# A kernel for a two-layer decoder trunk: the weights of the down and output products begin 128 bytes further on

## The chip, the cores and the metric

The kernel runs on 1 core of one Trainium2 chip. The metric is the device time of one execution in microseconds (us), as the median of several runs. A change within 0.2%, 1.2 us here, can't be told from none.

## What is computed

Two layers of a decoder over 256 tokens of 1024 numbers. Layer 0 mixes the tokens by stick-breaking attention, layer 1 by block-sparse attention with rotary positions (with 256 tokens its one block is plain causal attention). Behind each stands a squared-ReLU MLP. Cut to what matters here:

```python
def squared_relu_mlp(x, w1, w2):
    return jnp.square(jax.nn.relu(x @ w1)) @ w2

for i in range(DEPTH):                      # 2
    ln1_g, ln1_b, w1, w2, ln2_g, ln2_b = channel[i]
    h = layer_norm(DEEPNORM_ALPHA * h + mixers[i % N_MIXERS](h), ln1_g, ln1_b)
    h = layer_norm(DEEPNORM_ALPHA * h + squared_relu_mlp(h, w1, w2), ln2_g, ln2_b)
```

Each mixer ends in `merge_blocks(o) @ w_o`, the output projection. w1 is 1024 x 4096, w2 is 4096 x 1024, w_o 1024 x 1024, all float32.

## The kernel before, in words

Each float32 operand is split into a high and a low part (float32r), and a product is three matmuls into one accumulator: high by high, high by low, low by high (mm3, line 193). A matmul holds a block of 128 x 128 of one operand in the array, the weights, or stationary operand (sta), and streams the other, the moving operand (mov), past it. In the trace a matmul reads out<-moving,stationary.

All weights of the model come as units of 128 x 4 x 512 (1 MB): SyncE's queue loads a unit into a raw tile, ScalarE casts it to hi, VectorE subtracts to get lo (split, line 202). Which role hi and lo play depends on the product:

- Query and key products of layer 0 (qkT_ps) and six of eight chunks of the first MLP matrix (up_ps, up, line 638) run in projT (line 329): the weights are slices of hi and lo, the moving operand is xh or xl, 256 tokens, 256 columns.
- The other projections (v_ps, qk_ps, and two chunks of up_ps) run in proj (line 322): the weights are slices of xh and xl, the moving operand is hi or lo, 512 columns.
- The output projection (wo_ps, wo, line 596) takes its weights from oh and ol, the attention's output, and the down products with the second MLP matrix (dn_ps, down, line 670) theirs from hh and hl, the squared hidden values. The moving operand is hi or lo, 512 columns; only the last 24 matmuls of the kernel stream 256 columns.

hh, hl, oh and ol are the tiles of the pool st (line 167), three buffers of 4096 bytes per partition under each of two tags. A stationary slice is 128 numbers, 512 bytes per partition, and all slices of a tile lie a multiple of 512 bytes apart, so they all begin at the same place modulo 512. So do the moving slices, which are 1024 or 2048 bytes apart.

Pools lie behind one another in the order in which they are made, and a tile takes its size rounded up to 32 bytes. `shift` (line 215) puts an unused tile of a given size into the pool one; GAP (line 30) has its two sizes, 224 ahead of xh and 288 behind v. The layout that comes of it, as the first byte modulo 512:

| tiles | begins at, modulo 512 | role |
|---|---|---|
| xh, xl, h, v | 352 | moving in projT, stationary in proj |
| const (the identity in it) | 416 | moving in transposes |
| raw, hi, lo | 416 | moving in proj, wo, down; stationary in projT |
| ten buffers of t2k (qk, r, and others) | 416, 448, 480, 0, 32, 64, 96, 128, 160, 192 | stationary in transposes and scores |
| four buffers of t3k | 224, 256, 288, 320 | stationary in transposes |
| pt | 352 | moving in the attention's last product |
| st: hh, hl, oh, ol | 352 | stationary in down and wo |
| small tiles sm, sma | various | scalars per row |

The order of all instructions is fixed while the program is built by Plan (line 64), a small model that gives each operation a cost and emits it where its engine is free first. Its costs are constants per size; it knows no address. In the MLP the loop at line 698 takes up(c) and down(c - 2) in turn: 96 matmuls of 256 columns, then 48 of 512.

Of the kernel before, what the change touches and what calls it, by code (L numbers as in the profile page):

```python
# [7 lines left out]
F32 = mybir.dt.float32  # L8
# [6 lines left out]
P = 128  # L15
# [11 lines left out]
SEQ = (("A0", "V0", "A1", "A2", "A3", "V1"), ("A0", "A1", "V0", "A2", "A3", "V1"))  # L27

RAWS, LIVE = 3, 5
GAP = (224, 288)  # L30
N2K, N3K, NPT = 10, 4, 4
MARGIN, WINDOW = 0.5, 0.25
X_LOADS = {0: 1, 1: 1, 2: 2, 4: 2, 6: 2}
# [121 lines left out]
def trunk(ctx: ExitStack, tc: tile.TileContext, x, xt, cst, cstb, w, ln, out):  # L155
    nc = tc.nc

    def pool(name, bufs, **kw):
        return ctx.enter_context(tc.tile_pool(name=name, bufs=bufs, **kw))
# [4 lines left out]
    t2k = pool("t2k", N2K)  # L164
    t3k = pool("t3k", N3K)
    pts = pool("pts", NPT)
    st = pool("st", 3)
    small = pool("small", 4)
    smalla = pool("smalla", 8)
# [45 lines left out]
    def shift(n):  # L215
        one.tile([P, n // 4], F32, tag=f"gap{n}", name=f"gap{n}")

    shift(GAP[0])
    xh = one.tile([P, KT, T], F32R, tag="xh", name="xh")
    xl = one.tile([P, KT, T], F32R, tag="xl", name="xl")  # L220
    h = [one.tile([P, D], F32, tag=f"h{t}", name=f"h{t}") for t in range(NT)]
    v = [one.tile([P, D], F32, tag=f"v{t}", name=f"v{t}") for t in range(NT)]
    shift(GAP[1])

# [584 lines left out]
```

## Time and profile before

| | |
|---|---|
| median of 3 runs | 604.55 us (604.28 to 605.46) |
| profiled execution | 603.84 us, span 602.1 us |
| busy: TensorE, its weight loads, VectorE, ScalarE, GpSimd | 98%, 84%, 65%, 48%, 4% of the span |
| the chain that ended last | 95% TensorE |
| mean granted clock of TensorE | 0.995 |
| read from HBM | 107.71 MB, 181 GB/s over the span |

The profile is of one execution. Engines are named PE (TensorE, its matmuls), PEld (its weight loads), DVE (VectorE), ACT (ScalarE), POOL (GpSimd), SP (SyncE). L191 is line 191 of the kernel, and since mm records every matmul of the projections there, they are told apart by tiles. A matmul's record lasts longer than its turn, for matmuls are pipelined: what a matmul costs in a stream is the time from its start to the next one's start.

### The profile page before, as it was taken

What the parts mean: (1) busy time and instruction counts of PE and PEld (TensorE: products, weight loads), DVE (VectorE), ACT (ScalarE), POOL (GpSimd) and SP (SyncE); (2) the same over time, 40 slices, a digit from 0 to 9 for tenths busy, and PEclk for the clock granted to TensorE, in tenths of its full rate; (3) what the DMA queues carried; (4) which work ended last, traced back from release to release, by engine and by line L of the source; (5) the groups of instructions that cost most, each with busy time, mean ns of one, the idle gap of its engine ahead of it and who ended that gap; (6) DMA issues with size and microseconds to landing.
All of it is one profiled execution on the core that took longest, in us unless ns stands there. A gap on an engine that the chain in (4) does not pass through costs nothing.

```text
span 602.1 us, 8790 instructions
## 1 busy us (share of the span) xinstructions
PE 591.5 (98%) x3652; PEld 507.1 (84%) x3652; DVE 389.7 (65%) x492; ACT 290.5 (48%) x419; POOL 24.6 (4%) x30
## 2 busy tenths in 40 slices
PE   8999999999999999999999999999999999999994
PEld 6899987879899899898877777778798998899883
DVE  5877874878455554655879787668667537446454
ACT  5866663436443543642536655626346426435400
POOL 0000000000000000000122022000000000000000
PEclk9999999999999999999999999999999999999998
DMA  8994335185546337337274443443764464365101
GB/s 310 393 334 143 126 154 200 70 277 169 215 179 269 149 143 279 140 144 275 71 249 170 145 144 132 140 141 101 249 260 162 149 270 169 157 235 209 72 0 70
DMA packets 17895, 109.31 MB, mean 182 GB/s; under 512 B 1984, under 2 KB 2624, under 8 KB 5824
## 3 DMA queue, kind: packets, MB, share of 16 engines
q1 hardware_dynamic: 17856, 108.76, 49.0%
q8 instruction: 28, 0.46, 0.3%
q14 instruction: 11, 0.09, 0.0%
HBM read 107.71 MB, written 1.05 MB: 181 GB/s over the span
## 4 chain that ended last, share of the span: by engine, by line
PE 95%; DVE 2%; ACT 1%; DMA 1%; SPq 0%; issue 0%; DVEq 0%; ACTq 0%
PE dn_ps L191 29%; PE up_ps L191 28%; PE wo_ps L191 7%; PE v_ps L191 7%; PE qk_ps L191 7%; PE qkT_ps L191 7%; PE sc L191 3%; PE o L509 2%; PE xt L387 1%; PE tp L556 1%; DMA h<-in_xt 1%; DVE lo L206 1%; DVE xl L206 1%; PE ht_ps L663 1%; PE pt_ps L491 1%; PE pt_ps L493 1%
## 5 line engine op out<-in xcount | busy, mean ns | idle before, releaser
L206 DVE TENSOR_TENSOR lo<-raw,hi 128x1024 fp32r<-128x1024 f32 (+1 forms) x196 | 229.7, 1213 | 48.8 <-ACT hi L205 47.1
L205 ACT CAST hi<-raw 128x1024 fp32r<-128x1024 f32 (+1 forms) x196 | 192.0, 1032 | 64.2 <-issue 42.4
L191 PE MATMUL up_ps<-xh,hi 128*128 128x256 f32 x384 | 106.4, 277 | 0.0
L191 PE MATMUL up_ps<-xl,hi 128*128 128x256 f32 x384 | 106.2, 276 | 0.0
L191 PE MATMUL up_ps<-xh,lo 128*128 128x256 f32 x384 | 106.1, 276 | 0.0
L191 PE MATMUL dn_ps<-hi,hl 128*128 128x512 f32 (+1 forms) x260 | 101.5, 390 | 0.0
L191 PE MATMUL dn_ps<-lo,hh 128*128 128x512 f32 (+1 forms) x260 | 101.0, 388 | 0.0
L191 PE MATMUL dn_ps<-hi,hh 128*128 128x512 f32 (+1 forms) x260 | 100.2, 385 | 0.0
L191 PEld LDWEIGHTS up_ps<-xl,hi 128*128 128x128 f32 x384 | 72.1, 188 | 0.5
L191 PEld LDWEIGHTS up_ps<-xh,hi 128*128 128x128 f32 x384 | 72.1, 188 | 0.5
L630 DVE SCALAR_TENSOR_TENSOR r<-up_ps,r 128x512 f32<-128x512 f32 x32 | 22.0, 688 | 78.0 <-ACT r L628 78.0
L191 PEld LDWEIGHTS up_ps<-xh,lo 128*128 128x128 f32 x384 | 72.2, 188 | 0.0
L628 ACT ACTIVATE r<-up_ps 128x512 f32<-128x512 f32 x32 | 19.1, 596 | 95.0 <-PE up_ps L191 95.0
L191 PEld LDWEIGHTS dn_ps<-lo,hh 128*128 128x128 f32 x260 | 48.8, 188 | 10.5
L191 PEld LDWEIGHTS dn_ps<-hi,hh 128*128 128x128 f32 x260 | 48.8, 188 | 10.0
L191 PEld LDWEIGHTS dn_ps<-hi,hl 128*128 128x128 f32 x260 | 48.9, 188 | 9.4
L191 PE MATMUL qkT_ps<-xh,hi 128*128 128x256 f32 x128 | 36.8, 287 | 0.0
L191 PE MATMUL qkT_ps<-xh,lo 128*128 128x256 f32 x128 | 35.8, 280 | 0.2 <-DVE lo L206 0.2
L191 PE MATMUL qkT_ps<-xl,hi 128*128 128x256 f32 x128 | 35.7, 279 | 0.0
L205 ACT CAST xh<-xt 128x512 fp32r<-128x512 f32 x12 | 7.0, 587 | 42.9 <-PE xt L387 41.1
L191 PE MATMUL v_ps<-hi,xh 128*128 128x512 f32 x64 | 26.4, 413 | 0.0
L191 PE MATMUL qk_ps<-hi,xh 128*128 128x512 f32 x64 | 26.3, 411 | 0.0
(97 smaller groups left out, 885.8 us busy)
## 6 DMA issues: line engine op xcount, KB each, us to landing
raw<-in_w SPq DMA_DIRECT2D x64, 1024.0 KB, 5.0
raw<-in_wqkv SPq DMA_DIRECT2D x22, 1024.0 KB, 5.2
raw<-in_wo SPq DMA_DIRECT2D x8, 1024.0 KB, 4.8
raw<-in_first SPq DMA_DIRECT2D x8, 256.0 KB, 4.8
gb<-in_l_ln_g SPq DMA_DIRECT2D x4, 512.0 KB, 4.0
gb<-in_l_ln_b SPq DMA_DIRECT2D x4, 512.0 KB, 5.8
h<-in_x SPq DMA_DIRECT2D x2, 512.0 KB, 7.7
h<-in_xt SPq DMA_DIRECT2D x3, 256.0 KB, 4.8
```

Of the source, the lines that this page charges most:

```text
L191: nc.tensor.matmul(ps, sta, mov, start=start, stop=stop)
L205: f = lambda: nc.scalar.copy(hi(), src())
L206: g = lambda: nc.vector.tensor_tensor(lo(), src(), hi().bitcast(F32), op=ALU.subtract)
L387: nc.tensor.transpose(XB[t][:, n, k * P:(k + 1) * P], h[t][:, (4 * n + k) * P:(4 * n + k + 1) * P], ident)
L491: nc.tensor.transpose(ps[:, j, 0:P], pj[:, T:T + P], ident)
L493: nc.tensor.transpose(ps[:, j, T:T + P], pj[:, P:T], ident)
L509: nc.tensor.matmul(o[HD * j:HD * j + HD, 0, kt * P:T], v[kt][:, hd * HD:(hd + 1) * HD], pt[:, 0:T] if kt == 0 else pt[:, T:T + P], start=k ...
L556: nc.tensor.transpose(tb["tp"][:, pr, c0:c0 + P], QK[g, t]["qk"][:, e * T + pr * P:e * T + pr * P + P], ident)
L628: nc.scalar.activation(box["r", n], ps, AF.Relu)
L630: return dve(512, lambda: nc.vector.scalar_tensor_tensor(box["r", n], ps, 0.0, box["r", n], op0=ALU.max, op1=ALU.mult), after=[a], rank=0. ...
L663: nc.tensor.transpose(box["ht"][:, 0, k * P:(k + 1) * P], box["r", 0][:, k * P:(k + 1) * P], ident)
```

## The change

A pool of one tile of 128 bytes per partition, never read or written, is made ahead of st. So hh, hl, oh and ol begin at 480 instead of 352 modulo 512 bytes, 128 bytes further on; sm and sma, which lie behind st, move by 128 bytes too. Everything else stays where it was.

```diff
-GAP = (224, 288)
+GAP = (224, 288, 128)
...
     pts = pool("pts", NPT)
+    pool("gap", 1).tile([P, GAP[2] // 4], F32, tag="gap", name="gap")
     st = pool("st", 3)
```

## Rows read from the trace of the kernel before

**Rows 1.** The page: busy time by engine, and the chain by engine and line.

```profile
PE 591.5 (98%) x3652; PEld 507.1 (84%) x3652; DVE 389.7 (65%) x492; ACT 290.5 (48%) x419; POOL 24.6 (4%) x30
...
PE 95%; DVE 2%; ACT 1%; DMA 1%; SPq 0%; issue 0%; DVEq 0%; ACTq 0%
PE dn_ps L191 29%; PE up_ps L191 28%; PE wo_ps L191 7%; PE v_ps L191 7%; PE qk_ps L191 7%; PE qkT_ps L191 7%; PE sc L191 3%; PE o L509 2%; PE xt L387 1%; PE tp L556 1%; DMA h<-in_xt 1%; DVE lo L206 1%; DVE xl L206 1%; PE ht_ps L663 1%; PE pt_ps L491 1%; PE pt_ps L493 1%
```

**Rows 2.** Chain in order of time, 153 to 290 us: start us, us, what.

```profile
164.86 10.91 PE up_ps L191 x96
175.76 10.98 PE dn_ps L191 x48
```

**Rows 3.** Busy time by stretch; columns in the first line.

```profile
core 0: us, PE busy (x) PEld busy (x) DVE busy (x) ACT busy (x) POOL busy (x), PEclk, DMA share, GB/s
153.90:164.80 10.90, 10.90 (x49) 8.93 (x48) 7.22 (x8) 6.61 (x9) 0.00 (x0) 1.00 0.37 134
164.90:175.70 10.80, 10.80 (x97) 10.80 (x96) 4.63 (x4) 3.26 (x4) 0.00 (x0) 1.00 0.72 276
175.80:186.70 10.90, 10.90 (x49) 8.94 (x48) 7.22 (x8) 6.61 (x9) 0.00 (x0) 1.00 0.31 113
```

**Rows 4.** TensorE in order of time, a down block: start us, us, line, operation.

```profile
175.60 0.39 PE L191 MATMUL dn_ps<-hi,hh 128*128 128x512 f32 x1
...
176.29 0.39 PE L191 MATMUL dn_ps<-hi,hh 128*128 128x512 f32 x1
176.51 0.39 PE L191 MATMUL dn_ps<-lo,hh 128*128 128x512 f32 x1
...
177.66 0.39 PE L191 MATMUL dn_ps<-hi,hh 128*128 128x512 f32 x1
```

**Rows 5.** Groups of down and output matmuls by shape: busy us, mean ns | idle us.

```profile
L191 PE MATMUL dn_ps<-hi,hl 128*128 128x512 f32 x252 | 99.3, 394 | 0.0
L191 PE MATMUL dn_ps<-lo,hh 128*128 128x512 f32 x252 | 98.8, 392 | 0.0
L191 PE MATMUL dn_ps<-hi,hh 128*128 128x512 f32 x252 | 98.0, 389 | 0.0
...
L191 PE MATMUL wo_ps<-lo,oh 128*128 128x512 f32 x64 | 25.1, 392 | 0.0
```

**Rows 6.** TensorE in order of time, an up block.

```profile
165.63 0.28 PE L191 MATMUL up_ps<-xh,lo 128*128 128x256 f32 x1
...
175.49 0.28 PE L191 MATMUL up_ps<-xh,lo 128*128 128x256 f32 x1
```

**Rows 7.** TensorE in order of time, the last down matmuls.

```profile
592.95 0.28 PE L191 MATMUL dn_ps<-hi,hl 128*128 128x256 f32 x1
...
593.63 0.28 PE L191 MATMUL dn_ps<-hi,hl 128*128 128x256 f32 x1
```

**Rows 8.** TensorE from 142.28 us; groups by shape, 142.3 to 144.6 and 36.5 to 45 us.

```profile
142.28 0.28 PE L191 MATMUL up_ps<-xh,hi 128*128 128x256 f32 x1
142.40 0.28 PE L191 MATMUL up_ps<-xl,hi 128*128 128x256 f32 x1
...
L191 PE MATMUL up_ps<-xh,lo 128*128 128x256 f32 x6 | 1.7, 281 | 0.0
...
L191 PE MATMUL qkT_ps<-xl,hi 128*128 128x256 f32 x25 | 7.0, 281 | 0.0
```

**Rows 9.** Groups at 376.15 us, then at 139.04 us, one matmul each.

```profile
L191 PE MATMUL v_ps<-hi,xl 128*128 128x512 f32 x1 | 0.4, 401 | 0.0
...
L191 PE MATMUL up_ps<-hi,xl 128*128 128x512 f32 x1 | 0.4, 392 | 0.0
```

**Rows 10.** Tiles sm and r: count, ns shortest/median/longest, first and last start.

```profile
L366 POOL TENSOR_TENSOR sm<-sm,one x8: 985/986/992, 107.4 to 596.1; 128x1 f32<-128x1 f32 x8
...
L628 ACT ACTIVATE r<-up_ps x32: 590/597/605, 123.1 to 562.9; 128x512 f32<-128x512 f32 x32
...
L663 PE MATMUL ht_ps<-const,r x32: 270/272/273, 129.9 to 442.7; 128*128 128x128 f32 x32
```

## The prediction

> **What bounds the kernel now.** I read the page first. TensorE is busy for 98% of the span, and the chain of work that ended last lies on it for 95% [rows 1]. The same rows name the lines: the down products (tile dn_ps) hold 29% of the span and the output projection (wo_ps) 7%, and these two are the only places whose weights the change moves. The chain in order of time [rows 2] shows the rhythm of the MLP: a block of 96 up matmuls in 10.91 us, a block of 48 down matmuls in 10.98 us, ten such pairs in the kernel, with no other engine between them. There a nanosecond on a matmul is a nanosecond at the end. The table by stretch [rows 3] shows a granted clock of 1.00 in these blocks, the level of 2.4 GHz, so nothing in what follows is a clock that fell.
>
> So the question is the pace of one matmul, from its start to the start of the next. In a down block [rows 4] ten matmuls start from 175.60 to 177.66, nine steps in 2.06 us, 228.9 ns each; a whole block gives 10.98 us / 48 = 228.75 ns [rows 2], and I use 228.8. The steps are not even. The three kinds of a triple have records of 389, 392 and 394 ns in the mean [rows 5]; a record outlasts its step by a constant (391.7 in the mean less 228.8 is 163 ns), so the steps are about 226, 229 and 231 ns, which the starts show as 0.22 or 0.23. An up matmul has half the columns. From 165.63 to 175.49 [rows 6] there are 87 steps in 9.86 us, 113.3 ns each. Twice that is 226.7: for the same columns, a down matmul takes 2.1 ns more than two up matmuls.
>
> What differs? While a matmul streams its moving operand, the weights of the next are loaded, hidden behind it: TensorE's idle time before these groups is 0.0 [rows 5]. By the layout (section on the kernel), in a down or output product those weights begin 64 bytes **below** the moving operand modulo 512, 352 against 416. In an up product they begin 64 bytes **above** it, 416 against 352. The change gives the down and output products the relation of the up products: 480 against 416. That is the one thing in this trace which the change copies.
>
> **The change part by part.**
>
> *Instructions.* Nothing is added, removed or put in another order. The planner's costs know no address, and on all five engines the new program lists the same operations with the same waits. The gap tile has no instruction, so no queue and no DMA is touched.
>
> *The moved weights.* They are 252 x 3 = 756 down matmuls of 512 columns and 64 x 3 = 192 output matmuls [rows 5], 948 in all. The last 24 down matmuls have 256 columns and run at the up pace already, six steps from 592.95 to 593.63, 113 ns each, with the weights 64 below [rows 7]; I cost them at nothing. For the 948 the trace holds no matmul of 512 columns in the new relation, so I bound its price from both sides. On the side of a gain: the up pace, 228.8 - 226.7 = 2.1 ns, x 948 = 2.0 us. More can't be excluded; since the quickest step of the triple is 226 ns and no start in rows 4 shows a smaller one, I allow a second step of that size, 4.0 us, and no third. On the side of a loss: the relation 64 above has a slow pace too. The first up block of 256 columns begins at 142.28 with steps of 0.12 us and records of 281 ns instead of the 276 of the later up blocks, and a query projection of layer 0 has 281 ns in all three groups, 74 matmuls [rows 8]. Less the constant 163, that is 118 ns, 4.7 over the good pace. If this comes once per weight load, a long matmul takes 226.7 + 4.7 = 231.4 ns, 2.6 more than now, x 948 = 2.5 us. If it comes per column, 2 x 118 = 236 ns, 7.2 more, 6.8 us. The farthest row is a single matmul of 512 columns at 375.95 behind which weights beginning at 480 are loaded (a transpose whose data lie in the buffer at 480 of the pool t2k): its record is 401 ns, and that of one at 138.85, followed by a buffer at 64, is 392 [rows 9]; 9 ns x 948 = 8.5 us. Between these ends I take the gain of 2.0 us, since it is nearest to the rows that are most alike: each of the new down blocks begins where an up block ends, and all ten up blocks of 96, which begin where a down block ends, come to 113.3 ns (10.91 / 96 = 113.6 with their first few steps in it [rows 2]).
>
> *A rule on the pace.* The row says 228.75 ns for 512 columns [rows 2]. The Trainium skill, page "TensorE: Matmul & The Clock Gate", section "Back-to-back issue gap", gives an isolated step of columns / 2.4 + 2.5 ns, which is 215.8 ns here; the trace disagrees by 13 ns. As an estimate from that page, a change that took all of it away would bring 948 x 13 ns = 12.3 us.
>
> *What else lies behind the gap.* The two pools of small tiles behind st move as well. Their operations are few and work on a few numbers per row (POOL's power on sm: 8 times, 985 to 992 ns [rows 10]); nothing. ScalarE and VectorE write the weights to the new offset. Writes show no preference: 32 relus write ten buffers with ten different offsets in 590 to 605 ns [rows 10]. So the casts and subtractions of hh, hl, oh and ol are costed at nothing; their cover is the block of matmuls beside them, 10.8 us long, of which ScalarE works at most 6.6 and VectorE 7.2 [rows 3]. Without that cover a cast of 15 ns more, the spread of the relus, would cost 15 ns.
>
> *What is late next.* A pair of blocks would shrink by 48 x 2.1 = 100 ns in 21.9 us, and the next weights would be wanted that much sooner. The DMA engines are busy for 31 to 72% of these blocks and the two splitting engines leave a third free [rows 3], so supply follows and the whole gain reaches the end.
>
> **Sum.** The profiled execution took 603.84 us, 602.1 of them the span; it lies 0.71 us (0.12%) under the median of the three runs, 604.55. Its own sum is 603.84 - 2.0 = 601.8. Against the median: 604.55 - 2.0 = **602.5 us**.
>
> **The rivals.**
>
> *Nothing happens.* The load of the weights and the moving stream do not disturb each other, and the 2.1 ns belong to the longer matmul. For it: the last 24 down matmuls run at 113 ns with weights 64 below [rows 7], just as the up products do with weights 64 above; and the transposes, whose data are the weights and begin at many offsets, have records of 270 to 273 ns everywhere [rows 10]. Against it: 24 matmuls are few, and a transpose streams 128 columns, no more than the next load has. The time is 604.55. The Trainium skill has this as a rule: the same page, section "Step-by-step: what each phase is for", says that TensorE has two independent read ports and that loading the next weights takes no read bandwidth from the running matmul. By that rule an address changes nothing; the trace agrees for the short matmuls and can't tell for the long ones.
>
> *Slower.* The long matmuls fall into the slow pace of 142.28. The mechanism: stream and load start together, 64 bytes apart, and meet in the same part of the memory again and again; nothing inside a block of 48 shakes them apart, as nothing did in the 74 of rows 8. It decides from the first matmuls of a block. Price 2.5 to 6.8 us, 8.5 by the single matmul at 375.95: 607.0 to 613.0. For it: the slow pace is seen only where weights lie 64 above, and the one long matmul that was followed by weights at 480 is slow. Against it: the ten steady up blocks.
>
> *More than forecast.* Two steps, 4.0 us: 600.5. No row shows a long matmul at that pace.
>
> *The change doesn't do what it says.* In the new layout the tiles of st begin at 480 and all before them where they were. No chance is left for this.
>
> **How the numbers follow.** Faster, with the second step in it: 0.43. Nothing: 0.27. Slower: 0.30. The likeliest case has a range of its own, 600.5 to 603.3 us, its upper end being where 0.2% begins: that is what a measurement of this kernel can tell from no change, 1.2 us or 1.3 ns per moved matmul. The range must hold the case of no change and most of the slower one. Its main prices give 607.0 and 611.4; I stop between them at 609.0, which leaves out 0.11 above, and at 600.4, which leaves out 0.06 below. Each case lies on its own side of the 0.2%, so the chances are theirs: 0.43, 0.27 and 0.30.
>
> **What would show it.** Right: down blocks of 48 in 10.88 us instead of 10.98, and records near 390 ns in all three kinds in place of 389, 392 and 394, with the output products alike and the up blocks still at 10.91. Wrong towards nothing: the same three means. Wrong towards slower: records of 395 and more, blocks of 11.1 us and more. Wrong altogether if the up or the query products, whose operands stay, carry the difference, or if TensorE begins to wait for weights.

## The result, and the profile after

The changed kernel takes 610.89 us (median of 3 runs, 610.53 to 612.01) against 604.55 (604.28 to 605.46): 6.3 us more, ratio 1.0105 with a 95% interval of 1.0079 to 1.0132. The forecast was 602.5 with a range up to 609.0, so sign and range are both missed. The profiled execution took 610.89 us, 609.1 of them the span (before: 603.84 and 602.1).

The page of the changed kernel, busy time and then the chain by engine, answers to [rows 1]:

```profile
PE 598.2 (98%) x3652; PEld 509.8 (84%) x3652; DVE 389.8 (64%) x492; ACT 290.4 (48%) x419; POOL 24.7 (4%) x30
...
PE 94%; DVE 2%; DMA 2%; ACT 1%; SPq 0%; issue 0%; DVEq 0%; ACTq 0%
```

The same 3652 matmuls keep TensorE busy 6.7 us longer (598.2 - 591.5), its weight loads, which run beside them, 2.7 us longer, and no other engine's time moves by more than 0.1 us. So the loss is pace on TensorE. The chain of the changed kernel in order of time, 150 to 300 us (start us, us, what), shows where; it answers to [rows 2]:

```profile
154.87 11.19 PE dn_ps L192 x48
166.06 11.31 PE up_ps L192 x96
177.38 11.20 PE dn_ps L192 x48
188.57 10.90 PE up_ps L192 x96
199.47 11.19 PE dn_ps L192 x48
210.66 11.31 PE up_ps L192 x96
...
233.17 10.90 PE up_ps L192 x96
...
255.26 11.31 PE up_ps L192 x96
```

Two things are new. Every down block takes 11.19 or 11.20 us instead of 10.98: (11.195 - 10.98) / 48 = 4.5 ns more per long matmul, 233.3 instead of 228.8. And **some up blocks, whose operands were not moved, take 11.31 us instead of 10.91**, 117.8 ns a matmul; the others are as before. In layer 0 these are the blocks that begin at 166.06, 210.66 and 255.26, in layer 1 those at 466.91, 511.51 and 556.11: six of ten.

The groups by shape of the changed kernel (busy us, mean ns | idle us) confirm the first term, against 394, 392 and 389 in [rows 5]:

```profile
L192 PE MATMUL dn_ps<-hi,hh 128*128 128x512 f32 x252 | 99.8, 396 | 0.0
L192 PE MATMUL dn_ps<-hi,hl 128*128 128x512 f32 x252 | 99.7, 396 | 0.0
L192 PE MATMUL dn_ps<-lo,hh 128*128 128x512 f32 x252 | 99.6, 395 | 0.0
```

The three kinds have become alike, as the forecast wanted, but at records of 395 or 396 ns and not near 390; less the constant of 163 that is 233 ns a matmul. The second term is seen in the starts of TensorE's matmuls, in the block that begins at 166.06 and in the one that begins at 188.57:

```profile
169.79 0.28 PE L192 MATMUL up_ps<-xh,hi 128*128 128x256 f32 x1
...
170.97 0.28 PE L192 MATMUL up_ps<-xl,hi 128*128 128x256 f32 x1
...
191.83 0.28 PE L192 MATMUL up_ps<-xh,hi 128*128 128x256 f32 x1
...
192.96 0.28 PE L192 MATMUL up_ps<-xl,hi 128*128 128x256 f32 x1
```

Ten steps lie between the two starts of either pair: 1.18 us (118 ns) in the first block and 1.13 us (113 ns) in the second, with the same instructions and the same operands. The table by stretch of the changed kernel (columns as in [rows 3]) rules out the clock and the supply:

```profile
154.87:166.06 11.19, 11.19 (x51) 9.03 (x50) 7.22 (x8) 6.66 (x9) 0.00 (x0) 1.00 0.37 141
166.06:177.38 11.32, 11.32 (x98) 11.32 (x97) 4.63 (x4) 3.28 (x4) 0.00 (x0) 1.00 0.68 259
188.57:199.47 10.90, 10.90 (x98) 10.90 (x97) 4.63 (x4) 3.29 (x4) 0.00 (x0) 1.00 0.69 265
```

The granted clock is 1.00 in all three, the level of 2.4 GHz, and the slow and the good up block have the same work of the other engines and the same DMA share beside them.

**The account.** With the starts of all matmuls set beside those of the kernel before, one by one, the 948 moved long ones take 3.9 us more, 3.3 in the down and 0.7 in the output products (4.1 ns each; a full 4.5 would be 4.3 us), and the six up blocks 6 x 0.40 = 2.4 us. Together that is the 6.3 us by which the medians differ. The spans of the two profiled executions differ by 7.0 us: the other 0.7 lies in the first stages, ahead of every moved operand, where the same 84 query matmuls begin at 35.78 us in the kernel before and at 36.46 in the changed one:

```profile
35.78 10.09 PE qkT_ps L191 x84
...
36.46 10.09 PE qkT_ps L192 x84
```

### The profile page after: what moved, and what is told of

Its sections match the earlier page's. It is cut to its first block, busy times and chain, and to the rows that moved or that the text cites. A ratio compares the mean times of both kernels' runs of the same rounds, so it can differ in the third digit from the quotient of the medians.

```text
span 609.1 us, 8790 instructions
## 1 busy us (share of the span) xinstructions
PE 598.2 (98%) x3652; PEld 509.8 (84%) x3652; DVE 389.8 (64%) x492; ACT 290.4 (48%) x419; POOL 24.7 (4%) x30
## 4 chain that ended last, share of the span: by engine, by line
PE 94%; DVE 2%; DMA 2%; ACT 1%; SPq 0%; issue 0%; DVEq 0%; ACTq 0%
PE dn_ps L192 29%; PE up_ps L192 28%; PE wo_ps L192 8%; PE v_ps L192 7%; PE qk_ps L192 7%; PE qkT_ps L192 6%; PE sc L192 3%; PE o L510 2%; DMA raw<-in_wqkv 1%; PE xt L388 1%; DMA raw<-in_first 1%; DVE lo L207 1%; PE tp L557 1%; DVE xl L207 1%; PE ht_ps L664 1%; PE pt_ps L492 1%
## 5 line engine op out<-in xcount | busy, mean ns | idle before, releaser
L207 DVE TENSOR_TENSOR lo<-raw,hi 128x1024 fp32r<-128x1024 f32 (+1 forms) x196 | 229.8, 1213 | 52.5 <-ACT hi L206 50.8
L192 PE MATMUL dn_ps<-hi,hh 128*128 128x512 f32 (+1 forms) x260 | 102.0, 392 | 0.0
```

Source lines behind the costliest of these rows:

```text
L192: nc.tensor.matmul(ps, sta, mov, start=start, stop=stop)
L207: g = lambda: nc.vector.tensor_tensor(lo(), src(), hi().bitcast(F32), op=ALU.subtract)
```

## The experiments

The theory after this result: the **distance** from the start of the moving operand to the start of the weights that are loaded next (their starting bytes, taken modulo some power of two) sets the pace of a matmul, and an up block can in addition keep a slow rhythm in which it was begun. Rivals: the absolute place 480; the small tiles behind st, which move too; something in the entry to a block. Distances below are the weights' start less the moving operand's. "Long" is 512 columns, "short" 256; the paces are from start to start.

**1. Same places, old distances.** All operands of the kernel before move up by 128 bytes, so st begins at 480 and the small tiles lie where the change puts them, but every distance is the old one.

```
-GAP = (224, 288)
+GAP = (352, 288)
```

> All operands of the matmuls move by the same 128 bytes: xh begins at 480, hi and lo at 32, and hh, hl, oh, ol at 480, as in the changed kernel, but their distance to the moving operand stays 64 below. Theory (the distance between the next weights and the moving operand decides): the pace of before, 228.8 ns per long matmul, median near 604.5 us. Rival (where the weights begin, 480, decides by itself): 233.3 ns in the down, the output and, since xh begins at 480 too, the other long products, 948 + 576 matmuls at 4.5 ns, near 611 to 613 us.

Measured: 604.24 us (10 runs), ratio to before 0.9997, interval 0.9987 to 1.0006. The chain of this kernel:

```profile
154.58 10.99 PE dn_ps L191 x48
165.57 10.91 PE up_ps L191 x96
```

Both blocks are as before, and so are all ten up blocks. Neither 480 nor the small tiles cost anything: it is the relation between the operands that does.

**2. A stray transpose ahead of each up block** of the changed kernel, written to a bank that the block then overwrites.

```
+            nc.tensor.transpose(ps[:, 0, 0:P], ident, ident)
```

> The changed kernel with one transpose of the identity, overwritten at once, ahead of each of the 12 up blocks of 256 columns. Theory (the up blocks run at 118 ns because they keep a rhythm that they begin with, which any stray matmul can shift): the six slow up blocks change their pace, and if the good one is hit everywhere they return to 10.9 us, 6 x 0.4 = 2.4 us less, for 12 x 0.11 = 1.3 us more, so near 609.8 us; if the slow one is hit everywhere, near 614. The pattern of slow, good, slow, good in any case goes. Rival (the up blocks are slow for something outside TensorE that recurs every second block, such as loads or writes): the same blocks stay slow, near 612.2 us.

Measured: 610.35 us, ratio 1.0102 (1.0087 to 1.0117). The chain of this kernel:

```profile
199.63 11.20 PE dn_ps L192 x48
210.82 0.11 PE up_ps L643
210.93 10.90 PE up_ps L192 x96
...
233.02 0.11 PE up_ps L643
233.13 11.31 PE up_ps L192 x96
```

The down blocks stay slow. All six up blocks that were slow are good now, and two of the four that were good, the fourth in either layer, are slow (233.13 here, 233.17 above). The slow up blocks are thus no property of their operands or their place: the same block goes either way, by how it is entered. The 0.11 us at each of 12 borders, 1.3 us, eats most of what four slow blocks fewer bring (4 x 0.40 = 1.6 us).

**3 to 5. Other distances for st.** The buffers of st are spread so that three distances take turns, block by block: +64, +128 and +192 in the first kernel; 256, -192 and -128 in the second; -64, -32 and 0 in the third. The edit of the first, against the changed kernel; the second has 320 as the last number of GAP besides, and the third starts from the kernel before, with PAD and FILL at 32 and 416:

```
+PAD, FILL = 64, 320
...
-    st = pool("st", 3)
+    sth = pool("sth", 3)
+    pool("fill", 1).tile([P, FILL // 4], F32, tag="fill", name="fill")
+    stl = pool("stl", 3)
+    def pair(a, b):
+        return tuple(p.tile([P, 4 * T + PAD // 4], F32R, tag=tag, name=name)[:, :4 * T].rearrange("p (k q) -> p k q", k=4)
+                     for p, tag, name in ((sth, "sh", a), (stl, "sl", b)))
...
-                HT[c] = (st.tile([P, 4, T], F32R, tag="sh", name="hh"), st.tile([P, 4, T], F32R, tag="sl", name="hl"))
+                HT[c] = pair("hh", "hl")
```

> The three buffers of hh and oh, and of hl and ol, begin 64, 128 and 192 bytes above the moving operand modulo 512, so one run shows three distances, block by block. Theory (distance decides): 233.3 ns for the blocks at 64 above, and paces of their own for the other two, constant within a block. Rival (a place in the program or small tiles decide): all blocks alike.

> As the run before, with 256, 320 and 384 bytes above (256, 192 and 128 below). Theory: paces of their own, constant within a block, and if two streams only disturb each other when near, 226.7 ns or less for the far ones. Rival: all blocks alike.

> The buffers of hh, oh, hl and ol begin 64 below, 32 below and level with the moving operand, modulo 512. The paces of the two maps before repeat after 256 bytes (64 below as 192 above, 64 above as 192 below, 128 above as 128 below). Theory (the distance modulo 256 decides): 228.8 ns at 64 below; level is the same as 256 above, 226.7 ns; 32 below lies between or has a pace of its own. Rival (the period is 512, as the change's words have it): level has another pace than 226.7, the slowest if two streams that read the same place disturb each other most.

Measured, one run each: 608.79, 609.59 and 608.59 us. The chain of the second of these kernels, with down blocks at -192, 256 and -128:

```profile
154.69 11.19 PE dn_ps L199 x48
...
177.19 10.90 PE dn_ps L199 x48
...
199.40 11.13 PE dn_ps L199 x48
```

And of the third, with down blocks at -32, -64 and 0:

```profile
154.06 11.20 PE dn_ps L198 x48
...
176.57 11.01 PE dn_ps L198 x48
187.57 11.31 PE up_ps L198 x96
198.88 10.88 PE dn_ps L198 x48
```

A down block follows its own distance: 11.19 us at -192 as at +64, 10.90 at 256 and 10.88 at 0, 11.13 at -128 (the exceptions, all at 192 or -64 in the first kernel, stand in the last section). Distances that differ by 256 give the same pace, so the period is 256 bytes and not the 512 in which the change is described. Of the five up blocks of 96 in layer 0, two are slow in the first of these kernels, four in the second and all five in the third, the one behind the block at -64 (187.57) included: the distance of the block before does not settle an up block's rhythm by itself.

**6. Everything at a distance of 256.**

```
-GAP = (224, 288, 128)
+GAP = (32, 480, 320)
```

> xh, xl and hh, hl, oh, ol all begin at 160, hi and lo at 416: every long and every short matmul of the projections and of the MLP lies 256 from its next weights. Theory (distance modulo 256 decides, zero is best): 226.7 ns for all 948 + 576 long matmuls, 1524 x 2.2 = 3.3 us less than before; if the short matmuls keep 113.3 everywhere, another 0.9 us less for about 200 slow ones in the first layer and in the first up blocks; near 600.2 us. Rival (up blocks turn slow behind a down block of 226.7 ns, as they did in the second map): 10 x 96 x 4.2 ns = 4.0 us more, near 604.5.

Measured: 610.89 us, ratio 1.0100 (1.0085 to 1.0115). The chain of this kernel:

```profile
178.41 10.91 PE dn_ps L192 x48
189.31 11.51 PE up_ps L192 x96
```

The long matmuls, those of the first MLP matrix and the projections included, are at 226.7 ns, the best seen; the short ones all run at 120.0, the worst. **What is best for 512 columns is worst for 256.**

**7. Only st at 256.**

```
-GAP = (224, 288, 128)
+GAP = (224, 288, 320)
```

> Only hh, hl, oh, ol move, to 160, 256 from the moving operand; xh stays at 352. Theory: 948 long matmuls at 226.7 ns, 2.1 us less than before, and all ten up blocks of 96 slow at 117.8 ns, since they keep the rhythm in which such a down block leaves TensorE, 4.0 us more: near 606.4 us. Rival (the up blocks were slow for another reason): up blocks at 113.4, near 602.4.

Measured: 606.80 us, ratio 1.0035 (1.0020 to 1.0049). The chain of this kernel:

```profile
176.49 10.88 PE dn_ps L192 x48
187.37 11.31 PE up_ps L192 x96
```

Here the forecast gain of the long matmuls is real: 226.7 instead of 228.8 ns, 948 x 2.1 = 2.0 us. But all ten up blocks are in the slow rhythm, 4.0 us, and the last 24 short down matmuls are at 120 ns. From the 604.73 us that the kernel before took beside it, the sum is 604.7 - 2.0 + 4.0 + 0.2 = 606.9.

**8. The other operands moved instead.** xh and xl go to 480, st stays 64 below.

```
-GAP = (224, 288, 128)
+GAP = (352, 160, 512)
```

> hh, hl, oh, ol stay 64 below as before; xh and xl move to 480, so that the other 576 long matmuls have their weights 64 above and the short up and query matmuls have theirs 64 below. Theory: 233.3 ns for the 576, 2.6 us more; the short matmuls at 64 below have only been seen at 113.3 (24 of them), so up blocks good: near 606.5 us in all, less some tenths for the first up blocks. Rival (the tiles of st, not the distance, are the sensitive ones): 604.5.

Measured: 611.93 us, ratio 1.0120 (1.0105 to 1.0135), a miss of 5 us. The chain of this kernel:

```profile
178.78 10.99 PE dn_ps L192 x48
189.77 11.31 PE up_ps L192 x96
```

The long products of the first stages, now at +64, run at 233.3 ns as expected. The short ones, at -64 now, were expected at the 113.3 of the last 24 down matmuls [rows 7] and ran at 117.8, all of them. So short matmuls have two paces at -64, as at +64.

**9. A grid of 32 bytes for the short matmuls.** In the kernel before, the five buffers of the splits are spread, so each unit of weights brings another distance.

```
+PAD, FILL = 32, 352
...
+    def padded(pl, tag, name):
+        return pl.tile([P, 2048 + PAD // 4], F32R, tag=tag, name=name)[:, :2048].rearrange("p (k q) -> p k q", k=4)
...
-                            self.hi = splits.tile([P, 4, 512], F32R, tag="hi", name=f"hi{i}")
-                            self.lo = splits.tile([P, 4, 512], F32R, tag="lo", name=f"lo{i}")
+                            self.hi = padded(splits, "hi", f"hi{i}")
+                            self.lo = padded(splits2, "lo", f"lo{i}")
```

> The kernel before, with the five buffers of the splits spread over a grid of 32 bytes: the short products (up, transposed query and key) then have weights that begin 64, 96, 128, 160 or 192 bytes above the moving operand, a new one each time the unit of weights changes; st stays 64 below. Theory (the distance between the start of the next weights and the start of the moving operand, modulo 256, sets the pace, of short matmuls too): the pace changes with the unit, at its border, and units at 64 or 192 above can run at 113.3 ns, the ones at 96 and 160 at 117 to 119, at 128 about 119. Rival (for short matmuls only the rhythm with which a block is entered counts): each up block keeps one pace over both of its units, whatever their distances. Time 604 to 610, since the long products of the first stages have new distances as well.

Measured, one run: 614.31 us, above the expected range. TensorE in order of time, over the border of two units at 542.74 us (the first at +128, the second at +64):

```profile
542.03 0.28 PE L195 MATMUL up_ps<-xh,lo 128*128 128x256 f32 x1
...
542.74 0.28 PE L195 MATMUL up_ps<-xh,lo 128*128 128x256 f32 x1
...
543.99 0.28 PE L195 MATMUL up_ps<-xl,hi 128*128 128x256 f32 x1
```

Six steps of 118 ns up to the border (0.71 us), eleven of 114 behind it (1.25 us). The pace changes with the unit, inside one block, so the distance counts for short matmuls too: 120.0 ns at 160, 117.3 to 118.7 at 96, 118.6 to 118.8 at 128. But 64 and 192 ran at 113.3 in some units and at 117.8 in others. No distance of this grid gives the good pace every time. One thing the expectation overlooked: the moving operand of the down products is a split too, so st does not stay 64 below it, and the down blocks take 11.05 to 11.21 us instead of 10.98. By the starts, the up products of 256 columns lose 4.7 us and the down products 2.7, most of the 10 us that this kernel takes more than the kernel before.

**10. High and low parts at different distances.** In the changed kernel the high parts (hh, oh) go to 256 below, the low parts (hl, ol) stay at +64.

```
-    st = pool("st", 3)
+    sth = pool("sth", 3)
+    pool("gap2", 1).tile([P, 320 // 4], F32, tag="gap2", name="gap2")
+    stl = pool("stl", 3)
```

> The changed kernel, with the high parts of the second MLP matrix's operand and of the output projection's at 160 (256 below the moving operand) and the low parts still at 480 (64 above). In a triple the weights loaded next are high, low, high: two of three steps load a high part, one a low part. If the pace of a step is set by the weights that are loaded during it, a third of the long products have the distance of 64 and two thirds that of 256: a mean between 226.7 and 233.3 ns, about 229 in equal shares, uneven by the kind of the triple. If one disturbed load puts the whole stream out of step, 233.3 as before. If the weights in use count instead, a third of 64 as well, but the slow step is another kind of the triple. Time 606.5 to 611.

Measured, one run: 606.35 us. Groups by shape of this kernel, 170 to 590 us:

```profile
L194 PE MATMUL dn_ps<-hi,hl 128*128 128x512 f32 x231 | 91.8, 397 | 0.0
L194 PE MATMUL dn_ps<-lo,hh 128*128 128x512 f32 x231 | 90.6, 392 | 0.0
L194 PE MATMUL dn_ps<-hi,hh 128*128 128x512 f32 x232 | 90.5, 390 | 0.0
```

By the starts, the three steps are 236, 229 and 228 ns in the mean; its down blocks take 11.10 us (the chain of experiment 12 has the same figure), 231.2 ns in the mean. The slow step is the one whose own weights are hl. During it hh at 256 is loaded; hl was loaded during the step before, which has 229. So the expectation's last case, by which the weights in use count, names the slow step, but the mean misses: two thirds at 226.7 and one at 233.3 would be 228.9. One load in three at +64 costs 4.5 ns over 226.7, two thirds of the 6.6 that three cost. All ten up blocks are good here. With all weights at one distance, the weights in use and those loaded next lie alike, so the other kernels can't tell which of the two counts: this run speaks for the weights in use, or for a load whose cost falls on the step behind it. Which of them it is stays open.

**11. A stray matmul of 64 columns in bf16** ahead of each up block, in the kernel of experiment 7.

```
+            nc.tensor.matmul(ps[:, 0, 0:64], identb, maskb[0].rearrange("p a b -> p (a b)")[:, 0:64], start=True, stop=True)
```

> The kernel with st 256 below the moving operand (long products at 226.7 ns, all up blocks at 117.8; 606.8 us) with one stray matmul of 64 columns in bf16 ahead of each of the twelve up blocks, written to the bank that the block then overwrites. Theory: the slow pace of an up block is a rhythm taken over from the block before; a stray matmul of another length breaks it, eight to ten blocks of 96 come back to 113.3 ns, 0.4 us each, against 12 stray matmuls at about 0.1 us: 603 to 605, and down blocks still at 226.7. Rival (the pace comes from the address that the down block leaves, or from nothing that a stray matmul changes): up blocks stay at 117.8 and the time goes to 607.5 to 608.

Measured: 608.17 us, ratio 1.0066 (1.0049 to 1.0083). The chain of this kernel:

```profile
176.45 10.90 PE dn_ps L192 x48
187.35 0.04 PE up_ps L643
187.40 11.39 PE up_ps L192 x96
```

All ten stay slow, and each border costs 0.12 us more (0.04 for the stray one, 0.08 in the block). The theory that any matmul of another length breaks the rhythm falls. It is not without effect, though: the first up block of layer 0 (142.5 us), whose first 21 matmuls run at 117.7 or 117.8 ns in each of the other kernels with the up products at +64, runs at 113.3 here.

**12 and 13. What decides the rhythm of the up blocks?** As in 10, with the high parts at 256 and the low ones 64 below, as in the kernel before (first diff); and the reverse (second diff). Both diffs are against experiment 10.

```
-    pool("gap2", 1).tile([P, 320 // 4], F32, tag="gap2", name="gap2")
+    pool("gap2", 1).tile([P, 192 // 4], F32, tag="gap2", name="gap2")
```

```
-GAP = (224, 288, 320)
+GAP = (224, 288, 512)
```

> The high parts of the second MLP matrix's operand and of the output projection's at 160 (256 below the moving operand), the low parts at 352 (64 below, as in the kernel before). The low parts are the weights of the last product of each triple, so also the last weights before an up block. Theory: a long product's pace lies between those of the two distances, 226.7 and 228.9 ns, and an up block takes its rhythm from the last weights before it, so all ten up blocks are at 113.3 ns as in the kernel before: 602.4 to 604.5. Rival (the rhythm comes from the pace of the down block as a whole): up blocks at 117.8, 606.4 to 608.5.

> The reverse: high parts at 352 (64 below), low parts at 160 (256 below). Theory (an up block takes its rhythm from the last weights before it, here 256 below, as in the kernel with all of st there): up blocks at 117.8 ns, long products between 226.7 and 228.9: 606.4 to 608.5. Rival (two thirds of the weights are where they were in the kernel before, and the rhythm follows the down block as a whole): up blocks at 113.3, 602.4 to 604.5.

Measured: 606.29 us, ratio 1.0035 (1.0022 to 1.0047), and 605.14 us, ratio 1.0016 (1.0007 to 1.0026). The chain of the first:

```profile
176.51 11.10 PE dn_ps L194 x48
187.60 10.90 PE up_ps L194 x96
```

And of the second:

```profile
176.54 11.03 PE dn_ps L194 x48
187.57 10.90 PE up_ps L194 x96
```

The theory fails in both halves. All ten up blocks are good in both kernels, where it had them good in the first and slow in the second, so the last weights before the block do not decide; nor do the two thirds of the weights at 256 in the first kernel make the blocks slow, as its rival had it. And the long matmuls do not lie between 226.7 and 228.9: they take 231.2 ns (11.10 / 48) and 229.8 (11.03 / 48). **256 and 64 below in one stream are slower than either by itself**; 256 and +64 (experiment 10) lay between the two.

What decides the rhythm of an up block stays open. With the up products at +64 and st at one distance it was good in all ten blocks at -64, good in four and slow in six at +64, slow in all ten at 256; with high and low parts at two distances it was good in all ten, three times; and a transpose ahead of a block can turn it. The starts show one thing more. In the changed kernel all six slow up blocks begin 229 or 230 ns after the last down matmul, all four good ones 235 or 236. The record of that matmul differs too, here at 165.85 us (slow block next) and at 188.36 us (good block next):

```profile
L192 PE MATMUL dn_ps<-hi,hl 128*128 128x512 f32 x1 | 0.4, 392 | 0.0
...
L192 PE MATMUL dn_ps<-hi,hl 128*128 128x512 f32 x1 | 0.4, 398 | 0.0
```

A down block behind a good up block ends the first way and one behind a slow block the second, so slow and good take turns. In the third kernel of experiments 3 to 5, three slow up blocks behind -64 begin after 226 or 227 ns and the one good one after 231, as the ten of the kernel before do (230 or 231). So it goes along with the point in its uneven steps at which the down block ends. No run set that point, and no one limit holds for every distance (behind 128 a block that begins after 234 ns is slow), so this is not shown to be the cause. No layout that was tried beats the kernel before.

The paces by distance modulo 256, of stretches of some 20 matmuls and more in which all loads have one distance (worked out from the starts in the traces):

| distance | long, ns | short, ns | seen in, among others |
|---|---|---|---|
| 0 (0, 256) | 226.7 | 120.0 | 4 to 7 |
| +64 (64, -192) | 233.3 | 113.3 or 117.8 | changed, 3, 4, 8, 9 |
| -64 (-64, 192) | 228.9 to 229.4, three stretches in 3 at 233.3 | 113.3 or 117.8 | before, 3, 5, 8, 9 |
| 128 (128, -128) | 232.0 to 232.2 in blocks of 48 | 118 to 119 | 3, 4, 9 |
| -32 | 233.3 | not tried | 5 |

## Why the prediction was wrong

- **What bounds the kernel** held. TensorE is the chain, no supply came late, the clock did not move, and a nanosecond on a matmul was a nanosecond at the end.
- **That the pace depends on where the weights begin** against the moving operand held, and experiment 1 shows it: same places, same small tiles, old distances, old time. That it is the weights loaded next, and not those in use, is not shown (experiment 10). The new places by themselves, waits and other engines cost nothing, as forecast.
- **The failed step is the price of the moved weights**: "Between these ends I take the gain of 2.0 us, since it is nearest to the rows that are most alike". The up products have the same distance but half the columns, and the pace does not carry over from one length to the other: at +64 a short matmul can run at 113.3 ns and a long one runs at 233.3, at 0 a short one runs at 120.0 and a long one at 226.7 (experiments 6 and 7). The term was -2.0 us and measured +3.9. The rows of 512 columns were set aside, and they were read short. The single long matmul followed by weights at 480 [rows 9] was slow, 401 ns, but it was not the only one: by the addresses in the program the matmul at 133.59, too, is followed by a transpose whose data lie at 480, and its record is 392 ns, as after most other buffers. Two more, followed by a buffer at 320, which is +64 modulo 256, have 401 ns. None of the four is faster than those after other buffers, so no row of this length spoke for a gain. The row that was missed:

```profile
133.59 0.39 PE L191 MATMUL up_ps<-hi,xl 128*128 128x512 f32 x1
```

- **"The up blocks still at 10.91" failed.** The prediction named the slow pace of an up block [rows 8], 118 ns, and took the ten steady blocks as evidence against it. The six slow blocks of the changed kernel run at just that pace. What the forecast lacked is that a block's rhythm can follow from the block before, so that work whose operands stay can change: 2.4 us, over a third of the loss. Under "What would show it" it is named as a sign that the whole reading is wrong; the reading was incomplete. Experiment 2 shows that the way of entry matters; the layouts of 7, 10, 12 and 13 leave the up products' operands alone, and all ten blocks go one way or the other.
- **The rivals.** "Nothing happens" fell: the same instructions at other addresses take 226.7 to 233.3 ns. The Trainium skill's page "TensorE: Matmul & The Clock Gate", section "Step-by-step: what each phase is for", has two read ports and a load that takes no read bandwidth from the running matmul. The prediction's conclusion from it, that an address changes nothing, does not hold here; what inside the chip makes the places matter, no run shows. "Slower" was right in sign. Its price per column, 611.4, lies 0.5 us from the result, but by luck: 7.2 ns on each moved matmul was 4.1, and the up blocks made up the rest. Its reason, that the slow pace is seen only with weights 64 above, does not hold either (117.8 ns at -64 in experiment 8).
- **The chances.** The slower case had 0.30 and a range cut at 609.0. The rows of the right length stood on the slow side or showed no change, none on the side of a gain, so the loss should have had more than the gain's 0.43 and the range should have reached its price of 611.4.

## What to carry to other kernels

In this kernel, where TensorE is the chain and its float32r matmuls run back to back, the offset between weights and moving operand modulo 256 bytes is worth up to 3% of a long matmul's pace (226.7 to 233.3 ns) and 6% of a short one's (113.3 to 120.0), and the good offset depends on the number of columns: price it by rows of the same length, and do not carry it from another. Read the blocks before and behind the moved ones too, since a rhythm can be handed on to work that was not touched. Try a mixed layout before trusting it: 256 and 64 below in one stream were slower than either.

## What the runs showed of the hardware that was not expected

- The pace goes by the distance with a period of 256 bytes, for long matmuls nearly always with one value for each distance. The exceptions are three stretches in experiment 3, which ran at 233.3 instead of 228.9 ns: a down block at 192 that begins at 476.74 us, 24 down matmuls at 192 from 581.6 and 27 of the next stage at -64 from 299.5. The last two follow long matmuls at +64 directly and keep their pace, so long matmuls can keep a rhythm as well. A down block at 192 of that kernel as usual, and the exception:

```profile
199.06 10.99 PE dn_ps L199 x48
...
476.74 11.20 PE dn_ps L199 x48
```

- Short matmuls at 64 either side have two paces, 113.3 and 117.8 ns, and the blocks of 96 whose weights all lie at one distance keep one of them from about their sixth matmul to their end.
- With high and low parts at two distances, the slow step is the one whose own weights lie at +64, not the one during which they are loaded (experiment 10), and mixing 256 with -64 adds 1 to 2.4 ns to the mean over the kernel before (experiments 12 and 13: 229.8 and 231.2 against 228.8).
